# Moving the modulation rows of layer 1 out of the pair stages of a hybrid diffusion block's MLP

## The chip, the cores and the metric

The kernel runs on one core of a Trainium2 chip. The metric is the device time of one execution in microseconds (us); lower is better.

## The reference, cut to what matters

Two layers work on 512 latent tokens of width 1024. Each layer computes six modulation vectors of the conditioning vector, applies a mixer and then an MLP with squared ReLU. All of it is in 32-bit floats.

```python
for i in range(DEPTH):                      # DEPTH = 2
    mod_l = split(silu(c) @ ada_w[i] + ada_b[i], 6)          # 6 x 1024 numbers per layer
    a_lat = rmsnorm(h_lat, norm1_g[i]) * (1 + mod_l[1]) + mod_l[0]
    y_lat = mixer_i(a_lat)                  # i = 0: attention and long convolution; i = 1: pooling
    h_lat = h_lat + mod_l[2] * y_lat
    n = rmsnorm(h_lat, norm2_g[i]) * (1 + mod_l[4]) + mod_l[3]
    h_lat = h_lat + mod_l[5] * (square(relu(n @ mlp_w1[i])) @ mlp_w2[i])
return rmsnorm(h_lat, final_g)
```

The change concerns `mod_l` of layer 1: 6 x 1024 numbers, each a dot product of 1024 terms.

## The kernel before, in words

Tokens lie along the free dimension and channels on the 128 partitions, so that an activation of 1024 channels is eight tiles of 128x512. Every product of 32-bit numbers is made of rounded high parts and remaining low parts: high by high, high by low, low by high. So each weight tile of 128x1024 is loaded (`raw`, L182), rounded to its high part (`whi`, on ACT, L165) and subtracted to give its low part (`wlo`, on POOL in four pieces at L171, or on DVE in one at L173).

**The MLP** (`mlp`, from L1646) runs in each layer over four blocks of 1024 hidden channels, `blk` 0 to 3. A block has a *first map* (activations by `w1`, eight output tiles f = 0 to 7, squared ReLU in between) and a *second map* (by `w2`, eight output tiles d = 0 to 7, each added to the residual stream by `h_add`, L1582, with the gate `mods[layer, 5]`).

- In block 0 the first map has four tiles in halves and then four *whole tiles* f = 4 to 7 (`proj`, 24 matmuls of 512 columns). Its second map also makes sums of the activations (`act_sums`, L1657: five steps on DVE, one sum and four low parts on POOL, for d = 0 to 3), which blocks 1 to 3 use.
- In blocks 1 to 3 the first map is done in four *pairs* (`pair7`, L1721): two output tiles from seven half-size products instead of eight, with sums of two weight tiles in place of some tiles. A pair has 84 matmuls of 256 columns (L1681, L1682 and L1684). `pair_sums` (L1433; L1439 and L1440) makes weight sums on DVE, `pair_first` (L1446) others on POOL, and `pair7` itself asks DVE for the low part of one more weight (`w2 = w_split(..., dve)`), which PE needs in the fourth product.
- The second map of block 3 is `residual_norm` (L1598): four whole tiles, then four in halves, with the next norm's sums of squares beside them.

**Weights** are numbered k in the order of their use. `w_next` (L1477) fetches up to k + 7 and prepares up to k + 2; `w_more` does one ahead. Even k take a buffer of the ring `sraw` (four buffers), odd k one of `traw` (three).

**Modulation rows.** A row is one 128x1024 slice of layer 1's modulation matrix: `g_fetch` (L1489) loads it (512 KB, issued by SP at L1494) into a buffer of the same ring `sraw`, `grow` (L1499) multiplies it with the broadcast silu(c) and sums along the row (DVE, L1511, then a read of the accumulator), and `ada_fin` adds the bias (L254) or forms the scale (L249), in one more small DVE step. There are 48 rows, eight per vector, in the order of the six vectors (`gq`). `grow` has at most one row in flight beyond the one that it works on, and `glim` says up to which row it may go.

Nothing reorders the instructions: each engine does them in the order of the program text, SP too. An SP load whose buffer is still in use holds up all loads behind it. Before the change all 48 rows stand in layer 0's MLP: 8 in block 0's second map (two after each of d = 4 to 7), one after each pair of blocks 1, 2 and 3, and 14 in each of the second maps of blocks 1 and 2 (two after d = 0 to 5, one after d = 6 and 7).

Of the kernel before, what the change touches and what calls it, by code (L numbers as in the profile page):

```python
# [93 lines left out]
def body(ctx: ExitStack, tc: tile.TileContext, I, out):  # L94
# [1326 lines left out]

    pairs, first_done, sums_done, scr = set(), set(), set(), [None]

    def w_split(k, src, eng, n=1024):
# [35 lines left out]
    def w_prep(n):  # L1462
        while len(wsp) < min(n, len(wsrc)):
            k = len(wsp)
            if k in pairs:
                pair_first(k)
                wsp.append(w_split(k, wraw[k], pool))
            elif k - 1 in pairs:
                pair_sums(k - 1)
                wsp.append(w_split(k, scr[0][:, : 2 * T], dve))  # L1470
            else:
                eng = (dve, pool)[k // 2 % 2]
                wsp.append(wload(None, pool if k in fast else eng, "st"[k % 2], wraw[k]))

    wk = [0]
# [18 lines left out]
            nc.sync.dma_start(out=g, in_=I["adaT"][layer, c * D + j * P : c * D + (j + 1) * P, :])  # L1494
            gin.append(g)

    gk, glim = [0], [len(gq)]

    def grow(n=1):  # L1499
        for _ in range(n):  # L1500
# [97 lines left out]
    def residual_norm(kh, kl, gate, nrm, mod_a, d0=0, hook=None, late=0):  # L1598
# [3 lines left out]
        for d in range(d0, 4):  # L1602
            w = w_next()
            pp = ps_m("r")
            proj(pp, w, kh, kl, late=late if d == d0 else 0)
            h_add(d, 0, T, pp, gate)
            if hook and d == d0 + 1:
                hook()
            while fin:
                fin.pop(0)()  # L1610
            fin.append(nrm.add(d, 0, T))
# [34 lines left out]
    def mlp(layer, ah_, al_, nrm, i_norm, shift_in, last_norm, mod_next, load=None, seven=True):  # L1646
# [3 lines left out]
        if seven:  # L1650
            th = ml.tile([P, 4, 2, 3, 256], F32R, name=nm("th"), tag="pth")
            scr[0] = ml.tile([P, 2048], F32, name=nm("scr"), tag="ptl")
            pairs.update(k0 + 16 * blk + f for blk in (1, 2, 3) for f in (0, 2, 4, 6))


# [29 lines left out]
        for blk in range(4):  # L1685
# [89 lines left out]
            if blk == 0:  # L1775
# [21 lines left out]
                wait = pair(0, n, {16: mid0, 28: mid1} if layer == 0 else {48: mid0})  # L1797
                wait += pair(2, n, {} if layer == 0 else {8: mid1})
                steps(gb_[0])
                for f in range(4):  # L1800
                    w = ws[f]
                    pp = f_tile(f)
                    proj(pp[:, :n], w, ah_, al_, 256, n)
                    wait.append(lambda f=f, pp=pp: f_out(f, 256, n, pp))
                    wait.pop(0)()
                    w_more()
                while wait:
                    wait.pop(0)()
            if blk and seven:
                fin7 = lambda part: None  # L1810
                glim[0] = min(gk[0] + 4, len(gq))
                for f in range(0, 8, 2):
                    while len(gin) < min(gk[0] + 1, glim[0]):
                        g_fetch()
                    fin7 = pair7(f, fin7)
                    grow()
                fin7(3)
            else:
                for f in range(f0, 8):
                    w = w_next()  # L1820
                    pp = f_tile(f)
                    proj(pp, w, ah_, al_)
                    f_out(f, 0, T, pp)
            if blk < 3:
                glim[0] = min(gk[0] + (8 if blk == 0 else 14), len(gq))
                for d in range(ND):
                    if d == (0 if blk else 3):
                        while len(gin) < min(gk[0] + 2, glim[0]):
                            g_fetch()
                    w = w_next()  # L1830
                    pp = ps_m("r")
                    proj(pp, w, gh, gl, late=2 if blk and seven and d == 0 else 0)
                    h_add(d, 0, T, pp, gate)
                    if seven and blk == 0 and d < 4:
                        act_sums(d)
                    grow((0 if d < 4 else 2) if blk == 0 else (1 if d > 5 else 2))
            else:
                residual_norm(gh, gl, gate, last_norm, mod_next, hook=load, late=2 if seven else 0)

# [328 lines left out]
```

## Time and profile before

| what | value |
|---|---|
| time, median of 3 runs | 1125.92 us (1122.36 to 1126.22) |
| the profiled execution's own time | 1125.44 us |
| its span on the core, first to last instruction | 1123.6 us |
| mean granted TensorE clock | 0.987 of 2.4 GHz |
| PE (TensorE matmul) busy | 1068.5 us, 95% of the span |
| DVE (VectorE) busy | 792.2 us, 71% |
| POOL (GpSimd) busy | 677.5 us, 60% |
| ACT (ScalarE) busy | 522.6 us, 47% |

Times in the profile count from the first instruction. A row of a timeline gives start, duration, engine, line, operation, tiles and, in square brackets, how long the engine stood still just before and what ended it. PE's matmuls overlap, so that a row of one matmul is longer than the distance to the next. The chain of waits goes back from the last instruction through what released each step. A wait is put down to the instruction that came last.

### The profile page before, as it was taken

What the parts mean: (1) busy time and instruction counts of PE and PEld (TensorE: products, weight loads), DVE (VectorE), ACT (ScalarE), POOL (GpSimd) and SP (SyncE); (2) the same over time, 40 slices, a digit from 0 to 9 for tenths busy, and PEclk for the clock granted to TensorE, in tenths of its full rate; (3) what the DMA queues carried; (4) which work ended last, traced back from release to release, by engine and by line L of the source; (5) the groups of instructions that cost most, each with busy time, mean ns of one, the idle gap of its engine ahead of it and who ended that gap; (6) DMA issues with size and microseconds to landing.
All of it is one profiled execution on the core that took longest, in us unless ns stands there. A gap on an engine that the chain in (4) does not pass through costs nothing.

```text
span 1123.6 us, 17467 instructions
## 1 busy us (share of the span) xinstructions
PE 1068.5 (95%) x6604; PEld 942.8 (84%) x6604; DVE 792.2 (71%) x1258; ACT 522.6 (47%) x892; POOL 677.5 (60%) x723
## 2 busy tenths in 40 slices
PE   8899999999999999699999989999999999999996
PEld 5488888788989987688898888999878988988986
DVE  6689899999855547697798787386456934834843
ACT  4455245666544532273164155366433732732741
POOL 4457337885665449686596386476478834844822
PEclk9899999999999999899999999999999999999998
DMA  9776654225432323447736745521322341341302
GB/s 334 277 267 204 235 189 150 60 69 177 145 142 76 114 94 124 138 147 238 236 131 219 248 131 184 210 76 39 113 76 77 112 142 53 108 147 52 106 34 76
DMA packets 48664, 161.53 MB, mean 144 GB/s; under 512 B 5250, under 2 KB 8578, under 8 KB 48452
## 3 DMA queue, kind: packets, MB, share of 16 engines
q1 hardware_dynamic: 46132, 149.93, 39.6%
q0 software_dynamic: 2448, 10.49, 2.7%
q8 instruction: 52, 0.85, 0.3%
q14 instruction: 32, 0.26, 0.1%
HBM read 156.20 MB, written 4.20 MB: 143 GB/s over the span
## 4 chain that ended last, share of the span: by engine, by line
PE 57%; DVE 23%; DMA 8%; POOL 5%; issue 3%; ACT 3%; SPq 0%; POOLq 0%; ACTq 0%; DVEq 0%
PE r L206 7%; PE r L208 7%; PE r L212 7%; DMA g<-in_adaT 6%; PE f L1684 5%; PE f L1681 4%; PE f L1682 4%; DVE wlo L173 3%; DVE g L1511 3%; DVE g L638 3%; PE f L208 2%; PE f L212 2%; PE f L206 2%; DMA g<-in_adaN 1%; ACT whi L165 1%
## 5 line engine op out<-in xcount | busy, mean ns | idle before, releaser
L171 POOL TENSOR_TENSOR wlo<-raw,whi 128x256 fp32r<-128x256 f32 x308 | 265.1, 892 | 153.8 <-ACT whi L165 153.7
L206 PE MATMUL r<-gh,whi 128*128 128x512 f32 (+1 forms) x576 | 207.6, 369 | 1.6 <-ACT whi L165 1.5
L208 PE MATMUL r<-gl,whi 128*128 128x512 f32 (+1 forms) x576 | 207.0, 368 | 0.0
L165 ACT CAST whi<-raw 128x1024 fp32r<-128x1024 f32 x135 | 139.5, 1042 | 77.9 <-PE r L208 66.1
L1582 DVE SCALAR_TENSOR_TENSOR h<-r,mods,h 128x512 f32<-128x512 f32 (+1 forms) x81 | 54.0, 668 | 112.8 <-PE r L212 112.6
L212 PE MATMUL r<-gh,wlo 128*128 128x512 f32 (+1 forms) x576 | 132.0, 369 | 1.4 <-POOL wlo L171 1.4
L206 PEld LDWEIGHTS r<-gh,whi 128*128 128x128 f32 x576 | 108.3, 188 | 21.7 <-ACT whi L165 2.9
L208 PEld LDWEIGHTS r<-gl,whi 128*128 128x128 f32 x576 | 108.4, 188 | 18.6
L165 ACT CAST whi<-scr 128x1024 fp32r<-128x1024 f32 (+1 forms) x48 | 40.1, 835 | 175.7 <-DVE scr L1440 137.4
L212 PEld LDWEIGHTS r<-gh,wlo 128*128 128x128 f32 x576 | 100.2, 188 | 21.6 <-POOL wlo L171 3.0
L171 POOL TENSOR_TENSOR wlo<-scr,whi 128x256 fp32r<-128x256 f32 x48 | 60.4, 1278 | 74.0 <-ACT whi L165 51.3
L1681 PE MATMUL f<-nh,whi 128*128 128x256 f32 x384 | 95.3, 281 | 0.0
L1682 PE MATMUL f<-nl,whi 128*128 128x256 f32 x384 | 95.2, 281 | 0.0
L173 DVE TENSOR_TENSOR wlo<-raw,whi 128x1024 fp32r<-128x1024 f32 x58 | 73.8, 1272 | 13.9 <-ACT whi L165 13.9
L1511 DVE CUSTOM_DVE_ANT_0 g<-g,sbcl 128x1024 f32<-128x1024 f32 x48 | 63.5, 1323 | 21.7 <-DMA g<-in_adaT 21.6
L1681 PE MATMUL f<-th,whi 128*128 128x256 f32 x288 | 73.6, 287 | 3.1 <-ACT whi L165 3.1
L1682 PE MATMUL f<-th,whi 128*128 128x256 f32 x288 | 73.4, 286 | 0.0
L1681 PEld LDWEIGHTS f<-nh,whi 128*128 128x128 f32 x384 | 72.8, 189 | 0.2
L1682 PEld LDWEIGHTS f<-nl,whi 128*128 128x128 f32 x384 | 72.6, 189 | 0.3
L1684 PE MATMUL f<-th,wlo 128*128 128x256 f32 x288 | 49.4, 295 | 18.3 <-DVE wlo L173 18.2
L734 POOL TENSOR_TENSOR wlo<-raw,whi 128x1024 fp32r<-128x1024 f32 x17 | 43.1, 2533 | 38.3 <-ACT whi L725 37.9
L206 PE MATMUL u<-ah,whi 128*128 128x512 f32 x160 | 63.3, 396 | 1.1 <-DVE v L893 1.1
(415 smaller groups left out, 2812.1 us busy)
## 6 DMA issues: line engine op xcount, KB each, us to landing
raw<-in_w SPq DMA_DIRECT2D x128, 512.0 KB, 4.5
g<-in_adaT SPq DMA_DIRECT2D x80, 512.0 KB, 4.0
g<-in_adaN SPq DMA_DIRECT2D x16, 512.0 KB, 8.7
raw<-in_w_hy SPq DMA_DIRECT2D x12, 512.0 KB, 4.4
raw<-in_w_qk SPq DMA_DIRECT2D x8, 512.0 KB, 4.1
pth<-in_pth POOLq DMA_DIRECT2D x4, 768.0 KB, 9.1
raw<-in_w_out SPq DMA_DIRECT2D x5, 512.0 KB, 4.1
x<-in_xT SPq DMA_DIRECT2D x8, 256.0 KB, 7.2
```

Of the source, the lines that this page charges most:

```text
L165: act.copy(out=hi, in_=src)
L171: pool.tensor_tensor(out=lo[:, r], in0=src[:, r], in1=f32(hi)[:, r], op=ALU.subtract)
L173: (lo_eng or dve).tensor_tensor(out=lo, in0=src, in1=f32(hi), op=ALU.subtract)
L206: pe.matmul(ps, wh[:, c], ah[i][:, t0 : t0 + n], start=(i == 0), stop=False)
L208: pe.matmul(ps, wh[:, c], al[i][:, t0 : t0 + n], start=False, stop=False)
L212: pe.matmul(ps, wl[:, i * P : (i + 1) * P], ah[i][:, t0 : t0 + n], start=False, stop=(i == k - 1))
L734: ew(pool if k else dve).tensor_tensor(out=wts[k][1], in0=raws[k], in1=f32(wts[k][0]), op=ALU.subtract)
L1511: dve.tensor_tensor_reduce(out=gin[k], in0=gin[k], in1=sbc[0], scale=1.0, scalar=0.0, op0=ALU.mult, op1=ALU.add, accum_out=mods[:, layer, ...
L1582: dve.scalar_tensor_tensor(out=hs[d][:, seg], in0=pp[:, :n], scalar=gate[:, d : d + 1], in1=hs[d][:, seg], op0=ALU.mult, op1=ALU.add)
L1681: pe.matmul(o, l, b[i][0], start=(i == 0), stop=False)
L1682: pe.matmul(o, l, b[i][1], start=False, stop=False)
L1684: pe.matmul(o, w[1][:, c + i * P : c + (i + 1) * P], b[i][0], start=False, stop=(i == 3))
```

## The change

1. Rows no longer stand after pairs. Their places now are the whole tiles of block 0's first map (one after each of f = 4 to 7: the new `grow()` behind `f_out`), the second maps, and d = 0 to 3 of `residual_norm` (one each).
2. A helper `rows(n)` sets the limit to n more rows and starts the loads of the first two. In layer 0 it is called with 4 (before the halves of f = 0 to 3 in block 0), 8 (at d = 2 of block 0's second map, where it was d = 3), and 13, 13 and 4 (between the last pair of blocks 1, 2 and 3 and that pair's end). So layer 0 does 42 rows. The second maps of blocks 1 and 2 have two rows after d = 0 to 5, one after d = 6 and none after d = 7.
3. The last six rows go to layer 1's block 0: four beside its whole tiles, one after d = 0 and one after d = 1 of its second map. They belong to the gate, whose entries 2 to 7 are first read at d = 2 to 7 of that map.
4. `beside` names the first five weights of block 0's second map in each layer; their low parts are all on DVE. Before, POOL made two of them in layer 0 and three in layer 1.

```diff
+    beside = set()
...
-                eng = (dve, pool)[k // 2 % 2]
+                eng = dve if k in beside else (dve, pool)[k // 2 % 2]
...
-    gk, glim = [0], [len(gq)]
+    gk, glim = [0], [0]
+
+    def rows(n):
+
+        glim[0] = min(gk[0] + n, len(gq))
+        while len(gin) < min(gk[0] + 2, glim[0]):
+            g_fetch()
...
             proj(pp, w, kh, kl, late=late if d == d0 else 0)
             h_add(d, 0, T, pp, gate)
+            grow()
             if hook and d == d0 + 1:
...
             scr[0] = ml.tile([P, 2048], F32, name=nm("scr"), tag="ptl")
+            beside.update(range(k0 + 8, k0 + 13))
...
                 steps(gb_[0])
+                rows(4)
                 for f in range(4):
...
                 fin7 = lambda part: None
-                glim[0] = min(gk[0] + 4, len(gq))
                 for f in range(0, 8, 2):
-                    while len(gin) < min(gk[0] + 1, glim[0]):
-                        g_fetch()
                     fin7 = pair7(f, fin7)
-                    grow()
+                rows((13, 13, 4)[blk - 1])
                 fin7(3)
...
                     f_out(f, 0, T, pp)
+                    grow()
             if blk < 3:
-                glim[0] = min(gk[0] + (8 if blk == 0 else 14), len(gq))
                 for d in range(ND):
-                    if d == (0 if blk else 3):
-                        while len(gin) < min(gk[0] + 2, glim[0]):
-                            g_fetch()
+                    if blk == 0 and d == (0 if layer else 2):
+                        rows(8)
                     w = w_next()
...
-                    grow((0 if d < 4 else 2) if blk == 0 else (1 if d > 5 else 2))
+                    grow((layer if d < 4 else 2) if blk == 0 else 2)
```

Lines behind the first insertion move by 1 to 9 (L1511 is L1518 after the change, L1582 is L1589, L1439 is L1440).

**DVE, layer 0, from the last tiles of block 1's second map into the first pair of block 2.** `h` rows are `h_add`, `scr` rows are `pair_sums`, `ISA g` and `ISA mods` with the small step behind them are one modulation row, `wlo<-raw` behind them is the low part that PE's fourth product waits for. Before:

```order
L1439 TENSOR_TENSOR scr_3941<-raw_5508,raw_5468 128x512
L1440 TENSOR_TENSOR scr_3941<-scr_3941,raw_5468 128x512
L173 TENSOR_TENSOR wlo_5682<-scr_3941,whi_5681 128x1024
L1582 SCALAR_TENSOR_TENSOR h_3501<-r_5685,mods,h_3501 128x512
L1511 ISA g_5673,mods<-g_5673,sbcl 128x1024
L1511 ISA mods 128x1
L254 TENSOR_TENSOR mods<-mods,prm 128x1
L173 TENSOR_TENSOR wlo_5722<-raw_5508,whi_5721 128x1024
L1740 TENSOR_TENSOR r_5738<-f_5733,na_5735 128x256
```

And with the change:

```order
L1440 TENSOR_TENSOR scr_3941<-raw_5502,raw_5462 128x512
L1441 TENSOR_TENSOR scr_3941<-scr_3941,raw_5462 128x512
L173 TENSOR_TENSOR wlo_5674<-scr_3941,whi_5673 128x1024
L1589 SCALAR_TENSOR_TENSOR h_3501<-r_5677,mods,h_3501 128x512
L173 TENSOR_TENSOR wlo_5710<-raw_5502,whi_5709 128x1024
L1749 TENSOR_TENSOR r_5726<-f_5721,na_5723 128x256
```

The three rows of one modulation row between `h_add` and the low part are gone; the same holds at block 3 and behind every pair.

**DVE, layer 0, the last tile of block 0's second map and the first pair of block 1,** with the change:

```order
L1589 SCALAR_TENSOR_TENSOR h_3501<-r_4779,mods,h_3501 128x512
L1518 ISA g_4767,mods<-g_4767,sbcl 128x1024
L1518 ISA mods 128x1
L249 SCALAR_TENSOR_TENSOR smul<-mods,gpre,prm 128x1
L1518 ISA g_4805,mods<-g_4805,sbcl 128x1024
L1518 ISA mods 128x1
L249 SCALAR_TENSOR_TENSOR smul<-mods,gpre,prm 128x1
L173 TENSOR_TENSOR wlo_4818<-raw_4591,whi_4817 128x1024
```

Here nothing moved but the rows' numbers: before, two modulation rows stand at the same place, with L254 for L249, and the loads on SP around them stand in the same order too.

**DVE, layer 1, the first tile of block 0's second map.** `b` rows are `act_sums`. With the change:

```order
L1589 SCALAR_TENSOR_TENSOR h_3494<-r_8617,mods,h_3494 128x512
L1669 TENSOR_TENSOR b_8643<-nh_7993,nl_8001 128x512
L1671 TENSOR_TENSOR b_8645<-b_8643 128x256
L1672 TENSOR_TENSOR b_8645<-b_8644,b_8643 128x256
L1673 SCALAR_TENSOR_TENSOR b_8643<-b_8645,b_8643 128x256
L1674 SCALAR_TENSOR_TENSOR b_8644<-b_8643,b_8644 128x256
L1518 ISA g_8607,mods<-g_8607,sbcl 128x1024
L1518 ISA mods 128x1
L254 TENSOR_TENSOR mods<-mods,prm 128x1
L173 TENSOR_TENSOR wlo_8665<-raw_8487,whi_8664 128x1024
```

The last four rows are new on DVE at this place: before, the next `h_add` followed the five `act_sums` rows at once, and POOL made that low part ahead of its own `act_sums` steps.

## Rows read from the trace of the kernel before

**Rows 1.** The page, part 4: the chain that ended last, by engine.

```profile
PE 57%; DVE 23%; DMA 8%; POOL 5%; issue 3%; ACT 3%; SPq 0%; POOLq 0%; ACTq 0%; DVEq 0%
```

**Rows 2.** Stretches: length, busy us (instructions) of PE, weight load, DVE, ACT, POOL; clock, DMA, GB/s.

```profile
452.30:508.09 55.79, 44.10 (x337) 43.16 (x336) 46.03 (x69) 26.92 (x40) 39.97 (x37) 0.91 0.42 142
...
552.28:597.59 45.31, 40.76 (x337) 39.89 (x336) 41.36 (x62) 26.92 (x40) 35.52 (x32) 1.00 0.45 152
...
641.78:689.51 47.73, 42.62 (x337) 41.54 (x336) 42.20 (x66) 26.93 (x40) 35.01 (x32) 0.96 0.44 148
...
858.98:899.02 40.04, 40.04 (x337) 39.79 (x336) 32.79 (x49) 25.86 (x39) 36.09 (x36) 1.00 0.32 106
```

**Rows 3.** PE's waits (us in total, times, longest), layer 0's pairs of blocks 1, 2, 3.

```profile
PE f L1684 <- DVE wlo L173: 8.6, 3, 6.0
PE f L1681 <- ACT whi L165: 3.1, 1, 3.1
...
PE f L1684 <- DVE wlo L173: 4.5, 4, 1.6
...
PE f L1684 <- DVE wlo L173: 5.1, 4, 2.2
```

**Rows 4.** Timeline of DVE and PE, end of the third pair of block 1, layer 0.

```profile
500.14 1.45 DVE L1511 CUSTOM_DVE_ANT_0 g<-g,sbcl 128x1024 f32<-128x1024 f32 x1
502.12 1.21 DVE L173 TENSOR_TENSOR wlo<-raw,whi 128x1024 fp32r<-128x1024 f32 x1
...
503.39 0.73 PE L1684 MATMUL f<-th,wlo 128*128 128x256 f32 x4 [1.63 <-DVE wlo L173]
```

**Rows 5.** Timeline of DVE and PE where the pairs of blocks 2 and 3 begin.

```profile
555.88 1.54 DVE L1511 CUSTOM_DVE_ANT_0 g<-g,sbcl 128x1024 f32<-128x1024 f32 x1
557.95 1.21 DVE L173 TENSOR_TENSOR wlo<-raw,whi 128x1024 fp32r<-128x1024 f32 x1
...
559.22 0.74 PE L1684 MATMUL f<-th,wlo 128*128 128x256 f32 x4 [1.46 <-DVE wlo L173]
...
649.78 1.10 PE L1684 MATMUL f<-th,wlo 128*128 128x256 f32 x4 [2.15 <-DVE wlo L173]
```

**Rows 6.** Timeline of DVE, PE and SP's queue where the pairs of block 1 begin.

```profile
448.84 2.73 SPq L1494 DMA_DIRECT2D g<-in_adaT  x2
...
453.20 1.78 DVE L1511 CUSTOM_DVE_ANT_0 g<-g,sbcl 128x1024 f32<-128x1024 f32 x1 [1.38 <-DMA g<-in_adaT]
...
465.63 1.29 DVE L1511 CUSTOM_DVE_ANT_0 g<-g,sbcl 128x1024 f32<-128x1024 f32 x1 [3.18 <-DMA g<-in_adaT]
...
458.52 0.39 PE L1681 MATMUL f<-th,whi 128*128 128x256 f32 x1 [3.09 <-ACT whi L165]
...
468.70 1.22 PE L1684 MATMUL f<-th,wlo 128*128 128x256 f32 x4 [6.02 <-DVE wlo L173]
```

**Rows 7.** The page, part 5 (busy us, mean ns; idle before): low parts and rows on DVE.

```profile
L173 DVE TENSOR_TENSOR wlo<-raw,whi 128x1024 fp32r<-128x1024 f32 x58 | 73.8, 1272 | 13.9 <-ACT whi L165 13.9
L1511 DVE CUSTOM_DVE_ANT_0 g<-g,sbcl 128x1024 f32<-128x1024 f32 x48 | 63.5, 1323 | 21.7 <-DMA g<-in_adaT 21.6
```

**Rows 8.** DVE's waits in layer 1, 778 to 853 us: block 0, both maps.

```profile
DVE r L1699 <- ACT gh L1698: 16.4, 7, 4.2
DVE b L1663 <- POOL b L1661: 5.8, 2, 3.3
```

**Rows 9.** PE's wait in layer 1's block 0, second map, and DVE's idle time there.

```profile
PE r L206 <- ACT whi L165: 1.2, 1, 1.2
...
853.86 0.75 DVE L1582 SCALAR_TENSOR_TENSOR h<-r,mods,h 128x512 f32<-128x512 f32 x1 [3.02 <-PE r L212]
```

**Rows 10.** Timeline of DVE, layer 0's `residual_norm`, d = 2.

```profile
706.47 0.75 DVE L1582 SCALAR_TENSOR_TENSOR h<-r,mods,h 128x512 f32<-128x512 f32 x1 [4.77 <-PE r L212]
```

**Rows 11.** Timeline of DVE and POOL, layer 1's block 0, second map, a low part.

```profile
840.97 1.59 DVE L173 TENSOR_TENSOR wlo<-raw,whi 128x1024 fp32r<-128x1024 f32 x1 [1.48 <-ACT whi L165]
...
841.45 2.27 POOL L1661 TENSOR_TENSOR b<-nh,nl 128x512 f32<-128x512 f32 x1
```

## The prediction

> **What bounds the kernel now.** First the chain of waits, summed by engine: PE has 57% of the span and DVE 23% [rows 1]. PE is busy for 95% of the span, so a change can only win where PE stands still or runs at a low clock. Second, the windows cut at the stages that lose rows. The five pair stages shown do the same matmuls, 337 each [rows 2]. Layer 1's pairs, which have no modulation rows beside them, take 40.04 us, and PE is busy for all of it. Layer 0's, with a row behind each pair, take 55.79, 45.31 and 47.73. Taking 40.04 as the floor, the excess is 15.75 + 5.27 + 7.69 = 28.7 us, and this is the only room the pair stages offer. Third, who stopped PE there: nearly always L1684, PE's fourth product of a pair, waiting for DVE's low part at L173: 8.6, 4.5 and 5.1 us in the three blocks, plus one wait of 3.1 for ACT's high part [rows 3].
>
> The waits do not fill the whole excess. In block 2 the clock is 1.00 and PE's busy time is 40.76, 0.72 over the floor after four waits: a refill of 0.18 each. Block 1 has four waits too, and its busy time is 44.10: 4.06 - 0.72 = 3.3 us are left, which belong to a granted clock of 0.91 (part of the stretch at 1.2 GHz). Block 3: 42.62 - 40.04 - 0.72 = 1.9 us at a clock of 0.96. So block 1 pays 11.7 in waits, 0.7 in refills and 3.3 in clock; block 2 pays 4.5 + 0.7; block 3 pays 5.1 + 0.7 + 1.9.
>
> **The change, part by part.** *Rows leave the pairs.* At the end of block 1's third pair the low part starts at 502.12, and PE's product at 503.39 after 1.63 us of standing still [rows 4]. What ran on DVE just before it is a modulation row; where block 2 begins one can be measured, from 555.88 to 557.95: 2.07 us with its two small steps [rows 5]. Without the row the low part comes 2.07 earlier, as long as its high part is there (the bound is layer 1's stage, where the same program without rows has no wait). So each wait shorter than 2.07 goes, with its refill.
>
> - Block 2: the wait of 1.46 at its first pair [rows 5] came behind d = 7's row, which goes; the three behind pairs go too. All 4.5 + 0.7: **-5.3**, to the floor.
> - Block 3: its first pair's wait is 2.15 [rows 5], again behind d = 7's row; 0.1 stays. Block 2 waited 1.46 and kept its clock, so with 0.1 I expect block 3 to keep it: **-7.6**.
> - Block 1: its waits of 3.09 and 6.02 [rows 6] are another matter. They come behind d = 7's rows of block 0, which stay, in the same order on DVE. Two row loads left SP at 448.84; DVE waited 1.38 us for data at 453.20 and 3.18 at 465.63 [rows 6]. A load can only go when the buffer of an earlier row is free, and loads, rows and weights stand in the same order on SP after the change (the first two loads one tile earlier, at d = 2). I therefore leave both waits and the 3.3 of clock. Two steady waits go: 8.6 - 6.0 = 2.6, with 0.36 of refill: **-2.9**. The other end: all 15.75.
>
> *Where the rows go.* The second maps of blocks 1 and 2 have one row fewer and otherwise the same ones: 0. Six rows and three low parts come to DVE in layer 1's block 0. A low part is 1.27 on the mean [rows 7], so that is 6 x 2.07 + 3 x 1.27 = 16.2 us of new DVE work. DVE stood still there for 16.4 us in seven waits for ACT's squares, up to 4.2 each, and 5.8 for POOL's sums [rows 8]: 22.2 us of cover, and a row of 2.07 fits behind each whole tile. Without that cover it would be late for the next block. POOL loses three tiles, ACT's high part of d = 6 gets its buffer sooner, and the 1.2 us wait of PE [rows 9] goes with its refill: **-1.4**; the bounds are 0 and -1.4, and I take the upper gain because DVE still has 3.02 us of idle time before h_add at 853.86 [rows 9]. Four rows beside layer 0's whole tiles have the same cover as layer 1's: 0. Four in `residual_norm`: DVE idles 4.77 us before a tile's `h_add` [rows 10] against 2.07 of row: 0, or up to +3.3 if a wait there cost the clock as in block 1.
>
> A DVE low part took 1.59 us, against 1.27 on the mean, while POOL's sum of two 128x512 tiles at 841.45 took 2.27 [rows 11]. The Trainium skill (SBUF — State Buffer, Who interferes with whom) says that a DVE instruction with two SBUF inputs contends with a GpSimd instruction that reads SBUF, and that whoever issues second is blocked. By that rule the low parts and rows moved beside POOL's sums would stretch both engines, and layer 1's 1.4 could be lost: the sum would be 1.4 worse. The row agrees in direction, with 0.32 us.
>
> *SP.* Each row's load goes ahead of weight loads at three new places (whole tiles in either layer, `residual_norm`). I cost this at nothing, since weights are fetched seven ahead; if that cover were gone, block 1's entry shows the price (below).
>
> **Sum:** 5.3 + 7.6 + 2.9 + 1.4 = 17.2 us. From the profiled execution's 1125.44 that is **1108.2 us**. That execution lies 0.5 under the median of 1125.92, so the two starts are the same.
>
> **Rivals.**
>
> *Entries stay (1114.0).* The first pair of blocks 2 and 3 is late for another reason than the row, for example because d = 7's `h_add` itself comes late from PE. Then only the steady waits go: block 1's 2.9; block 2's 4.5 - 1.46 + 0.54 = 3.6; block 3's 5.1 - 2.15 + 0.54 = 3.5; layer 1's 1.4; together 11.4. For it: at the end of a map PE is the last to be done with d = 7. Against: the low part comes right behind a row, and the wait is about as long as one.
>
> *Block 1's entry goes too (1095.4).* Loads one tile earlier let rows run ahead, so the wait of 6.02 does not build up: 15.75 in place of 2.9. Against: the last loads still wait for the rows before them.
>
> *SP holds weights back (1148).* At each of the three new places a row load stuck on a buffer keeps the weights behind it, and PE waits as at block 1's entry: 3.1 + 6.0 + 0.36 + 3.3 = 12.8 us each, 38.4 in all against 15.8 gained in the pairs, so 22.6 slower. It ends slower once a place costs over 5.3. For it: block 1's entry is such a place, with eight rows. Against: there two rows stand behind each tile, here one.
>
> *DVE overflows in layer 1 (1129).* The 16.2 us find no cover and come out at the next block's entry with 3.3 of clock: 15.8 gained, 19.5 lost, 1129.1. The cover of 22.2 us speaks against it.
>
> *The change does not do what it says (1124).* If ACT's high part ends the wait rather than the row, the low part is no earlier and only layer 1's 1.4 comes. For it: DVE stood still 13.9 us for high parts in its low parts [rows 7]. Against: layer 1's pairs.
>
> **How the numbers follow.** My forecast has a chance of 0.64, with 1104 (a third of block 1's entry gained) to 1111.5 (`residual_norm` at its upper bound) as its own range. Entries stay: 0.16. Block 1's entry goes too: 0.08. SP holds weights: 0.04. DVE overflows: 0.02. The high part decides: 0.06. The first two together hold 0.80, so the range is 1101 to 1117, where the upper end is the second case with 3 us from `residual_norm`, and the lower the forecast with somewhat over half of block 1's entry. A measurement of this kernel tells about 0.5%, 5.6 us. Faster by more: 0.64 + 0.16 + 0.08 = 0.88. Within: 0.02 + 0.06 = 0.08. Slower: 0.04.
>
> **What would show it.** Right: layer 0's pair stages at about 53, 40 and 40 us; waits of L1684 for DVE's low part only at block 1's entry (about 6 us, behind ACT's 3.1) and at most 0.1 at block 3's; a granted clock of 1.00 in block 3 and below 1 in block 1; no wait of 1.2 us in layer 1's block 0; DVE's busy time higher and POOL's lower there. Wrong in its parts: waits of 1.5 to 2 us still at the first pairs of blocks 2 and 3 (entries stay); block 1 at 40 (the lower case); PE waiting for `whi` or DMA in a whole tile or in `residual_norm` (SP); a lag of `h_add` growing through layer 1's block 0, with a wait at its block 1 (overflow). Most of all the prediction is wrong if layer 0's pairs keep waits like the 1.63 us with no row before the low part.

## The result and the profile after

The changed kernel takes **1110.88 us** (median of 4 runs, 1108.43 to 1113.27), the kernel before in the same comparison 1124.79 (4 runs, 1122.36 to 1126.22): a ratio of **0.9878**, interval 0.9848 to 0.9909. The forecast was 1108.2, range 1101 to 1117. The profiled executions have spans of 1123.6 and 1110.1 us, 13.5 apart.

The windows of the changed kernel, with the columns of [rows 2]: layer 0's second map of block 0, its pairs of blocks 1, 2 and 3, its last map (`residual_norm` up to the halves), then layer 1's second map of block 0.

```profile
405.70:452.55 46.85, 45.47 (x194) 35.68 (x193) 35.22 (x52) 14.17 (x25) 34.61 (x33) 1.00 0.46 157
452.55:505.16 52.61, 43.50 (x337) 43.04 (x336) 40.33 (x60) 26.89 (x40) 35.32 (x37) 0.90 0.37 120
549.35:591.43 42.08, 40.83 (x338) 39.96 (x337) 36.38 (x55) 26.90 (x40) 32.31 (x32) 1.00 0.37 126
635.61:676.61 41.00, 40.52 (x337) 39.93 (x336) 36.02 (x54) 26.90 (x40) 32.23 (x32) 1.00 0.35 120
676.61:712.43 35.82, 35.45 (x206) 30.98 (x205) 19.04 (x31) 13.28 (x20) 22.76 (x29) 1.00 0.74 279
800.93:845.46 44.53, 44.44 (x194) 35.97 (x193) 34.27 (x47) 15.61 (x27) 32.60 (x32) 1.00 0.38 129
```

The kernel before, for the three maps that [rows 2] does not show:

```profile
405.21:452.30 47.09, 45.44 (x194) 35.66 (x193) 32.59 (x47) 14.18 (x25) 39.24 (x39) 1.00 0.38 123
689.51:724.43 34.92, 34.92 (x206) 30.85 (x205) 13.39 (x22) 13.36 (x20) 19.70 (x28) 1.00 0.65 238
812.90:858.98 46.08, 44.77 (x194) 35.89 (x193) 26.10 (x35) 15.73 (x27) 34.14 (x40) 1.00 0.20 69
```

Stage by stage, in us, against [rows 2] and these three:

| stage | before | after | difference | forecast |
|---|---|---|---|---|
| layer 0, block 0, second map | 47.09 | 46.85 | -0.24 | 0 |
| pairs of block 1 | 55.79 | 52.61 | -3.18 | -2.9 |
| pairs of block 2 | 45.31 | 42.08 | -3.23 | -5.3 |
| pairs of block 3 | 47.73 | 41.00 | -6.73 | -7.6 |
| last map of layer 0 | 34.92 | 35.82 | +0.90 | 0 |
| layer 1, block 0, second map | 46.08 | 44.53 | -1.55 | -1.4 |
| sum | | | -14.03 | -17.2 |

The first of these stages begins 0.49 us later in the profile of after (405.70 against 405.21), which makes the 13.5. Between profiles this point moves by some us: in those below it lies from 401.3 to 408.7. That arises ahead of all that the kernels place differently, since the stretch just ahead, which ends with the whole tiles, the first of those places, takes 33.5 us in each of them. So the experiments are read by the lengths of stages, and the medians beside them.

PE's waits in the three pair stages of layer 0, which answer to [rows 3]:

```profile
PE f L1693 <- DVE wlo L173: 6.0, 1, 6.0
PE f L1690 <- ACT whi L165: 3.1, 1, 3.1
...
PE f L1690 <- ACT whi L165: 0.8, 1, 0.8
PE f L1693 <- DVE wlo L173: 0.4, 1, 0.4
```

Block 1 keeps its two entry waits unchanged, and nothing else. Block 2 has a new wait, 0.8 for ACT's high part, and 0.4 for the low part; block 3 has a wait of 0.4 for the low part alone. All steady waits behind pairs are gone.

Where block 2 begins, on DVE and PE (timeline of after; the row of before that answers to the first stands last):

```profile
547.28 1.23 DVE L1518 CUSTOM_DVE_ANT_0 g<-g,sbcl 128x1024 f32<-128x1024 f32 x1 [4.71 <-DMA g<-in_adaT]
...
550.62 0.69 DVE L1440 TENSOR_TENSOR scr<-raw,raw 128x512 f32<-128x512 f32 x1
...
553.24 0.39 PE L1690 MATMUL f<-th,whi 128*128 128x256 f32 x1 [0.77 <-ACT whi L165]
...
556.61 0.75 PE L1693 MATMUL f<-th,wlo 128*128 128x256 f32 x4 [0.42 <-DVE wlo L173]
...
547.79 1.23 DVE L1511 CUSTOM_DVE_ANT_0 g<-g,sbcl 128x1024 f32<-128x1024 f32 x1 [2.53 <-DMA g<-in_adaT]
```

The second row of d = 5 waited 4.71 us for its data, where it had waited 2.53. Counted from the start of that map it ran 547.28 - 505.16 = 42.1 us in, against 547.79 - 508.09 = 39.7 before [rows 2]: 2.4 later. Behind it stand `h_add`, d = 6's row and `pair_sums`, on which ACT's high part waits. The rows ahead of it stand within 0.6 us of their old places. Its load left SP no later, 35.4 us behind the start of the map against 35.2 before, but the wait for it ended 6.7 us after it left, where that had taken 4.5. The two loads, after and before:

```profile
540.60 0.33 SPq L1495 DMA_DIRECT2D g<-in_adaT  x1
...
543.29 0.33 SPq L1494 DMA_DIRECT2D g<-in_adaT  x1
```

### The profile page after: what moved, and what is told of

It reads as the page before. It is cut to its first block, busy times and chain, and to the rows that moved or that the text cites. A ratio compares the mean times of both kernels' runs of the same rounds, so it can differ in the third digit from the quotient of the medians.

```text
span 1110.1 us, 17472 instructions
## 1 busy us (share of the span) xinstructions
PE 1066.5 (96%) x6604; PEld 941.5 (85%) x6604; DVE 797.0 (72%) x1263; ACT 522.1 (47%) x892; POOL 658.6 (59%) x703
## 4 chain that ended last, share of the span: by engine, by line
PE 60%; DVE 19%; DMA 11%; ACT 3%; POOL 3%; issue 3%; SPq 0%; POOLq 0%; ACTq 0%; DVEq 0%
DMA g<-in_adaT 8%; PE f L1693 7%; PE f L1690 7%; PE f L1691 7%; PE r L206 6%; PE r L208 6%; PE r L212 6%; DVE g L1518 3%; DVE g L638 3%; PE f L208 2%; PE f L212 2%; PE f L206 2%; DVE wlo L173 2%; DMA g<-in_adaN 1%; DVE h L1589 1%
## 5 line engine op out<-in xcount | busy, mean ns | idle before, releaser
L171 POOL TENSOR_TENSOR wlo<-raw,whi 128x256 fp32r<-128x256 f32 x288 | 246.9, 888 | 123.8 <-ACT whi L165 123.8
L1589 DVE SCALAR_TENSOR_TENSOR h<-r,mods,h 128x512 f32<-128x512 f32 (+1 forms) x81 | 54.0, 668 | 100.3 <-PE r L212 100.1
L171 POOL TENSOR_TENSOR wlo<-scr,whi 128x256 fp32r<-128x256 f32 x48 | 56.5, 1198 | 72.1 <-ACT whi L165 48.4
L173 DVE TENSOR_TENSOR wlo<-raw,whi 128x1024 fp32r<-128x1024 f32 x63 | 82.7, 1312 | 12.3 <-ACT whi L165 12.3
L1518 DVE CUSTOM_DVE_ANT_0 g<-g,sbcl 128x1024 f32<-128x1024 f32 x48 | 63.8, 1329 | 26.1 <-DMA g<-in_adaT 25.2
L208 PE MATMUL u<-al,whi 128*128 128x512 f32 x160 | 62.6, 391 | 0.0
```

Of the source, the lines that this page charges most:

```text
L171: pool.tensor_tensor(out=lo[:, r], in0=src[:, r], in1=f32(hi)[:, r], op=ALU.subtract)
L173: (lo_eng or dve).tensor_tensor(out=lo, in0=src, in1=f32(hi), op=ALU.subtract)
L208: pe.matmul(ps, wh[:, c], al[i][:, t0 : t0 + n], start=False, stop=False)
L1518: dve.tensor_tensor_reduce(out=gin[k], in0=gin[k], in1=sbc[0], scale=1.0, scalar=0.0, op0=ALU.mult, op1=ALU.add, accum_out=mods[:, layer, ...
L1589: dve.scalar_tensor_tensor(out=hs[d][:, seg], in0=pp[:, :n], scalar=gate[:, d : d + 1], in1=hs[d][:, seg], op0=ALU.mult, op1=ALU.add)
```

## Experiments

Two theories were on the table. **Work:** a row is 2 us of DVE work, and PE waits where it stands ahead of a low part. **Data:** DVE stands still ahead of a row because the row's load waited on SP for a buffer of the shared ring. They agree about pairs and differ about entries.

### early: four rows moved away from block 1's entry

```diff
-                rows(4)
+                rows(4 if layer else 6)
...
-                    grow()
+                    grow(2 if blk == 0 and layer == 0 and f < 6 else 1)
...
-                        rows(8)
+                        rows(8 if layer else 4)
...
-                    grow((layer if d < 4 else 2) if blk == 0 else 2)
+                    grow((layer if d < 4 else (2 if d < 6 else 0)) if blk == 0 else 2)
```

> The changed kernel, with the four rows of d = 6 and 7 in layer 0's block 0 moved: two go behind the whole tiles f = 4 and 5 of the same block, two to layer 1 (one after each of d = 0 to 3 there). Theory: block 1's entry (waits of 3.09 and 6.02 us and the low clock, 12.6 us over the floor of 40.0) comes from these rows, whose data arrive late in front of pair_sums and of the low part. Then both waits fall below 1 us, block 1's pair stage goes from 52.6 to 40 to 42 us, and the kernel to 1098 to 1101 us. Rival: the entry comes from pair_sums and the weights' own loads, whatever stands on DVE: then the pair stage stays over 50 us and the kernel at 1110. Second rival: DVE lags behind the whole tiles, with two rows there; then block 0's second map grows from 46.8 by over 2 us.

Measured: 1096.22 us, ratio 0.9741 (0.9705 to 0.9777). Layer 0's pairs of blocks 1 and 2 (block 3's take 40.01) and layer 1's second map of block 0:

```profile
452.01:492.56 40.55, 40.02 (x337) 39.77 (x336) 34.16 (x50) 26.90 (x40) 36.16 (x36) 1.00 0.34 118
536.74:577.18 40.44, 40.25 (x337) 39.81 (x336) 34.79 (x51) 26.88 (x40) 32.27 (x32) 1.00 0.34 118
...
783.94:829.29 45.35, 44.47 (x194) 35.97 (x193) 37.90 (x52) 14.54 (x26) 34.70 (x30) 1.00 0.45 150
```

Block 1 falls from 52.61 to 40.55 with the clock at 1.00: these four rows, with their loads, were its whole entry, waits and low clock. The rivals fall: the stage is not over 50 us, and block 0's second map stays at 46.8. The price: the two rows added behind d = 2 and 3 of layer 1 cost 0.8 there (45.35 against 44.53). Blocks 2 and 3 gained as well (42.08 to 40.44, 41.00 to 40.01), which the edit did not aim at. The entries thus depend on more than the rows that stand there.

### own_buffer: same order, other buffers

```diff
-            g = st.tile([P, D], F32, name=nm("g"), tag="sraw", bufs=4)
+            g = (ml.tile([P, D], F32, name=nm("g"), tag="gr", bufs=1) if k % 2 else
+                 st.tile([P, D], F32, name=nm("g"), tag="sraw", bufs=4))
```

> The changed kernel, in the same order, but every second row is loaded into a buffer of its own instead of the ring that it shares with the weights. Theory: what holds DVE at block 1's entry is less the rows' work than their loads, which wait for a buffer of the ring: DVE stood still 1.7, 1.8 and 3.2 us for row data there, 6.6 in all, against 9.1 us of waits of PE. Then these idle times shrink to 2 us or less in all, PE's two waits to 3 to 5 us, block 1's pair stage from 52.6 to 44 to 48, block 2's from 42.1 to 40 to 41, and the kernel to 1103 to 1107 us. Rival: the rows' work on DVE alone sets it, and an earlier load changes nothing: 52 to 53 us and 1110.

Measured: 1101.46 us, ratio 0.9782 (0.9751 to 0.9813). Block 0's second map, the pairs of blocks 1 and 2, the last map of layer 0; then DVE's waits for row data from 425 to 470 us, here and in the changed kernel:

```profile
402.49:450.68 48.19, 46.81 (x194) 36.79 (x193) 36.88 (x55) 14.18 (x25) 35.94 (x34) 0.96 0.47 150
450.68:498.04 47.36, 43.05 (x337) 42.39 (x336) 39.13 (x58) 27.19 (x40) 34.14 (x36) 0.93 0.39 132
542.22:581.93 39.71, 39.71 (x337) 39.66 (x336) 33.21 (x49) 25.67 (x39) 31.06 (x32) 1.00 0.39 141
665.81:700.73 34.92, 34.92 (x206) 30.85 (x205) 18.18 (x31) 13.12 (x20) 19.77 (x28) 1.00 0.72 265
...
DVE g L1519 <- DMA g<-in_adaT: 1.8, 1, 1.8
```

```profile
DVE g L1518 <- DMA g<-in_adaT: 6.6, 3, 3.2
```

DVE's idle time for row data falls by 4.8 us and block 1's pairs by 5.25, as the data theory has it. Block 2 goes to the floor (39.71 with PE busy throughout, 0.3 under the prediction's 40.04) and the last map back to 34.92: the 0.90 lost there were late data too. Block 0's map grew by 1.3 us, at a clock of 0.96 (the last section comes back to it). The 47.36 that is left in block 1 holds the rows' own work, the 1.8 us that DVE still waits for data, and the low clock (0.93): PE still waits 3.9 us for the low part and 0.4 for the high part. So at this entry both theories hold: about 5 us go to late data, and the 7 to 8 that are left were not split further.

### pair_rows_2: rows behind the pairs of block 2 again

```diff
                 fin7 = lambda part: None
+                if blk == 2:
+                    rows(4)
                 for f in range(0, 8, 2):
                     fin7 = pair7(f, fin7)
-                rows((13, 13, 4)[blk - 1])
+                    if blk == 2:
+                        grow()
+                rows((13, 9, 4)[blk - 1])
```

> The changed kernel with one part undone in one block: block 2 has a row behind each of its four pairs again, and its second map four rows fewer. Theory: a row of about 2 us between h_add or pair_sums and the low part makes PE's waits, as before the change: 0.5, 0.9 and 1.6 us return inside the stage with 0.18 us of refill each, and the stage goes from 42.1 to about 45.6 us; block 3's entry has fewer rows before it and loses its 0.4. Kernel 1113 to 1114. Rival: the pairs gained for another reason (POOL's lower load, loads of weights in time), and the stage stays within 0.5 us of 42.1.

Measured: 1113.24 us, ratio 0.9893 (0.9864 to 0.9921), 2.4 over the changed kernel; the intervals of the two ratios overlap, so the stages decide. Pairs of block 2 (block 3's take 39.74), and PE's waits there:

```profile
549.74:594.70 44.96, 41.24 (x337) 40.04 (x336) 40.98 (x63) 26.91 (x40) 35.37 (x32) 1.00 0.44 151
...
PE f L1693 <- DVE wlo L173: 3.7, 4, 1.6
```

The waits return, 1.6 the longest as in [rows 3, 4], and block 3 with four rows fewer ahead of it goes to the floor. Three of the four waits stand behind rows, 0.7, 0.9 and 1.6 us; none of these rows waited for its data. So work alone explains the steady waits.

### pool_low_parts: the change without its fourth part

```diff
-            beside.update(range(k0 + 8, k0 + 13))
```

> The changed kernel without its fourth part: the low parts of the first weights of block 0's second map are shared between DVE and POOL again, the rows stay where they are. Theory: the wait of 1.2 us in layer 1's block 0 went because POOL makes fewer low parts: it returns, and that map goes from 44.5 back to 46 us; layer 0's goes from 46.8 to about 47.1. Rows on DVE behind d = 0 and 1 may add to it, as POOL's low parts then come after the same sums: up to 48. Kernel 1111.5 to 1114. Rival: it went for another reason, and both maps stay within 0.3 us.

Measured: 1112.59 us, ratio 0.9892 (0.986 to 0.9924). Second maps of block 0, layers 0 and 1, and PE's wait in the second of them:

```profile
406.05:453.84 47.79, 45.45 (x194) 35.67 (x193) 35.56 (x50) 14.17 (x25) 41.65 (x40) 1.00 0.45 154
798.72:846.85 48.13, 46.09 (x194) 37.10 (x193) 31.93 (x45) 15.86 (x27) 36.20 (x40) 0.96 0.36 121
...
PE r L206 <- ACT whi L165: 2.0, 1, 2.0
```

Layer 1's map goes to 48.13, over the 46.08 of before: the wait of 1.2 [rows 9] comes back as 2.0, with the clock at 0.96. The fourth part is needed to place rows there; it is worth 3.6 us in layer 1 and 0.9 in layer 0 as the rows now stand. The median moves by 1.7 only, and the intervals of the two ratios overlap: in the profile block 2 has no entry wait here (its pairs take 40.2). The row load that took 6.7 us in the changed kernel took 5.1.

### d7_row: a row at d = 7 again

```diff
-                    grow((layer if d < 4 else 2) if blk == 0 else 2)
+                    grow((layer if d < 4 else 2) if blk == 0 else (1 if d in (0, 6, 7) else 2))
```

> The changed kernel with one row moved in each of the second maps of blocks 1 and 2: from d = 0 to d = 7, where a row stood before the change. Theory: the entries of blocks 2 and 3 are set by what stands on DVE behind d = 6 and 7; the row returns 1.5 to 2 us of wait there. Block 2's pair stage goes from 42.1 to 43.5 to 44.2 us, block 3's from 41.0 to 42.5 to 44.9 (the upper end with the clock falling as before the change), the kernel to 1113 to 1116. Rival: the entries shrank because the pairs before them no longer leave DVE behind, and the row at d = 7 costs under 0.5 us in each block.

Measured: 1117.41 us (10 runs, 1112.16 to 1123.12), ratio 0.9936 (0.9909 to 0.9962). Pairs of block 2 (block 3's take 44.40, at the same clock), and PE's wait there (the same in both):

```profile
548.35:592.70 44.35, 42.04 (x337) 41.38 (x336) 37.98 (x57) 27.02 (x40) 31.97 (x32) 0.96 0.38 129
...
PE f L1693 <- DVE wlo L173: 2.1, 1, 2.1
```

The low part's entry waits return, 1.7 more than the 0.42 of the changed kernel, and the clock falls as it did in block 3 before the change. That is what the prediction said of a row at d = 7. The kernel is over the expected 1116 for two stages more: `residual_norm`, 36.55 in place of 35.82, and block 0's map, 48.36 in place of 46.85. This map lies ahead of the edit and has the same instructions and waits as in the changed kernel; only its clock was lower, 0.96.

### before_own: the kernel before, with the other buffers

The edit is that of own_buffer, in the kernel before.

> The kernel before the change, rows at their old places, every second row in a buffer of its own. It tells whether places or loads made the loss. Theory: the steady waits behind pairs are DVE's work on a row and stay (0.9 and 1.6 in block 1, 0.5 to 1.6 in blocks 2 and 3); only the entry of block 1 gets shorter, by about 5 us as in own_buffer. Pair stages 50 to 51, 44.5 to 45.3 and 46 to 47.7 us; kernel 1118 to 1121. Rival: late loads make all of it, and an extra buffer would have done what the change does: pair stages of blocks 2 and 3 at 40 to 41 and the kernel at 1112 or less.

Measured: 1117.01 us (7 runs), ratio 0.992 (0.9896 to 0.9943). Pairs of blocks 1 and 2 (block 3's take 43.68) and PE's waits in block 2:

```profile
458.35:506.90 48.55, 42.21 (x338) 41.42 (x336) 43.04 (x66) 26.92 (x40) 38.11 (x35) 0.96 0.47 152
551.07:594.76 43.69, 40.51 (x337) 39.84 (x336) 40.45 (x61) 25.52 (x39) 35.52 (x32) 1.00 0.46 147
...
PE f L1685 <- DVE wlo L173: 3.2, 3, 1.6
```

The three steady waits stay, as expected. But the entries of blocks 2 and 3 are gone although d = 7's row stands there as before the change: with data in time DVE reaches it early enough. Together with d7_row: **late data and a row at d = 7 make these entries late together**. Without the late data nothing was left of them here; without the row most went, with stages of 42.08 and 41.00 in the changed kernel and 40.44 and 40.01 in early. More than the expected share of block 1's entry went as well (48.55), but block 0's map grew from 47.09 to 49.68 (the last section says why).

### early_own and early_own_low6: both edits together, and one low part more on DVE

early_own has both diffs; in the second kernel, besides:

```diff
-            beside.update(range(k0 + 8, k0 + 13))
+            beside.update(range(k0 + 8, k0 + 14))
```

> Both edits on the changed kernel: the four rows of d = 6 and 7 in block 0 moved (early), and every second row in a buffer of its own (own_buffer). Theory: the two take away the same entry waits in different shares and add up only in what is left. Against early, the pair stages of layer 0 lose 0.7, 0.7 and 0.3 us (to the 39.7 to 39.9 of layer 1), the last map of layer 0 0.3: 1093 to 1095 us, 1 to 3 under early. Rival: a new wait, the own buffer still held by the row two before, which DVE reaches late behind two rows in each of the whole tiles f = 4 and 5: then block 0's second map grows past 48.2, or weights come late, and the kernel is no faster than early (1096).

> As early_own, with one weight more in the list of those whose low parts DVE makes (six of block 0's second map in place of five), in both layers. Theory: PE's two waits of 0.4 and 0.9 us in layer 0's block 0, second map, are for low parts that POOL makes behind its own sums; with 3.0 us less on POOL ahead of them both go, and the map falls from 46.8 to 44.2 to 45.5 us; kernel 1 to 2.5 us under early_own. Rival: DVE, which makes sums there as well, holds the next high part's buffer longer, and a new wait of 1 us or more for ACT's high part comes in its place: no gain, or up to 2 us slower.

Measured: early_own 1101.02 us, ratio 0.9782 (0.9742 to 0.9821); early_own_low6 1095.28 us, ratio 0.972 (0.9673 to 0.9768). Block 0's second map of early_own, then PE's waits in it; the map of early_own_low6 last:

```profile
406.45:456.80 50.35, 48.31 (x194) 37.50 (x193) 36.80 (x52) 16.70 (x28) 38.10 (x37) 0.93 0.38 121
...
PE r L212 <- POOL wlo L171: 2.0, 3, 0.9
```

```profile
407.40:452.73 45.33, 44.72 (x194) 35.90 (x193) 36.64 (x52) 14.10 (x25) 32.29 (x30) 1.00 0.42 130
```

early_own was expected under early and came out 5 us over it (the intervals of the two ratios overlap, so the stages have to show why). All pair stages of layer 0 stand at the floor (39.73, 39.70, 39.70), but block 0's map grew from 46.8 to 50.35: a third wait for POOL's low part and the clock at 0.93. The named rival (a map past 48.2) came, though not through the rows of the whole tiles. The last section says what POOL did. One low part less for POOL brings the map to 45.33; as a kernel that is level with early.

### spread and spread_ring: no rows in layer 0's block 0 map

Beside early_own_low6: `rows(15)`, `rows(15)`, `rows(6)` in place of 13, 13, 4, no `rows` in layer 0's block 0 map, `grow(2 if d < 2 else 1)` in `residual_norm`. spread_ring has all rows in the shared ring.

> A version meant to be the best: as early_own_low6, but block 0's second map of layer 0 has no rows; its four go to the second maps of blocks 1 and 2 (15 each: two after d = 0 to 6, one after d = 7) and the two of layer 1 behind d = 2 and 3 to the last map of layer 0 (six: two after d = 0 and 1, one after d = 2 and 3). Theory: rows with their data in time cost only where DVE is late: block 0's map 44.2 to 45.3, no wait at block 1's entry (40.6 to 39.9), layer 1's map 44.5; the entries of blocks 2 and 3 stay without a wait although a row stands at d = 7, as in before_own: pair stages 39.7. Kernel 1090 to 1094, 1 to 4 under early_own_low6. Rival: 15 rows are one too many, d = 7's row returns waits of 1 to 2 us in both blocks (43 to 44 us each): 1097 to 1101.

> The same places as in spread, all rows in the ring that they share with the weights. It tells whether a row at d = 7 costs through its work or through late data. Theory from before_own (own buffer: entries of blocks 2 and 3 at no wait with a row at d = 7) and d7_row (ring: 2.15 in each): the data are late, so here blocks 2 and 3 have waits of 1.5 to 3 us at their entries and pair stages of 43 to 45 us, against 39.7 to 41 in spread; block 1's entry has no wait in either. Kernel 1098 to 1103. Rival: places alone decide, and both kernels have the same pair stages within 0.5 us.

Measured: spread 1102.02 us, ratio 0.9782 (0.975 to 0.9814); spread_ring 1107.05, ratio 0.9828 (0.9805 to 0.985). spread: block 0's map, the pairs of block 2 (block 3's take 41.88), the last map, and DVE's waits for row data from 491 to 540 us, block 1's map. spread_ring: the pairs of block 2 (block 3's take 44.57):

```profile
407.36:451.55 44.19, 44.19 (x194) 36.05 (x193) 29.98 (x41) 16.15 (x28) 31.14 (x33) 1.00 0.26 86
...
535.44:577.93 42.49, 40.29 (x337) 39.83 (x336) 37.08 (x57) 26.90 (x40) 32.33 (x32) 1.00 0.38 130
663.99:702.67 38.68, 35.56 (x206) 31.03 (x205) 21.32 (x37) 13.28 (x20) 22.14 (x29) 1.00 0.72 269
...
DVE g L1519 <- DMA g<-in_adaT: 1.8, 2, 1.6
```

```profile
531.57:577.79 46.22, 42.04 (x338) 41.38 (x336) 38.52 (x57) 27.04 (x40) 31.96 (x32) 0.96 0.39 127
```

The rival of the first came: 15 rows are one too many (42.49 and 41.88), and six in the last map cost 3.8 us. But the data were not in time everywhere, although every second row has its own buffer: the second row of d = 6 waited 1.6 us for them in block 1's map and 1.0 in block 2's, and three rows of the last map 9.3 together. So this cost is work and loads in one. In the shared ring blocks 2 and 3 take another 3.7 and 2.7 us. Block 0's map without rows is at 44.19, with no wait at all, and block 1's entry is gone.

### balanced and balanced_low5: each place loaded up to what it hides

Beside spread: 14, 14 and 4 rows in place of 15, 15 and 6; two rows in each of layer 0's whole tiles; six beside layer 1's whole tiles. The diff is against the changed kernel. balanced_low5 has five low parts on DVE, as the changed kernel.

```diff
-                rows(4)
+                rows(6 if layer else 8)
...
-                    grow()
+                    grow(2 if blk == 0 and (layer == 0 or f < 6) else 1)
...
-                    grow((layer if d < 4 else 2) if blk == 0 else 2)
+                    grow(layer if blk == 0 else (2 if d < 6 else 1))
```

> The version meant to be the best, after spread: every second row in a buffer of its own, six low parts on DVE, no rows in layer 0's second map of block 0; layer 0 has eight rows beside the whole tiles (two each), 14 in each of the second maps of blocks 1 and 2 (two after d = 0 to 5, one after d = 6 and 7, as before the change), four in the last map; layer 1 has six beside its whole tiles and one after d = 0 and 1. Theory: a place costs only where rows and their loads exceed what DVE has left before PE needs the next low part; 14 with the own buffer left no wait in before_own, 4 in the last map none in own_buffer. Against spread (1099.2 us of span) the pair stages of blocks 2 and 3 go from 42.5 and 41.9 to 39.7 and the last map from 38.7 to 34.9; all pair stages at 39.7 to 40.0, span 1090 to 1093, kernel 1091 to 1095. Rival: two rows in each whole tile overrun there, h_add lags and block 0's map of layer 0 grows by 2 us or more; then no faster than early (1096).

> As balanced, with five low parts on DVE, as in the changed kernel. It tells what made PE wait 0.4 and 0.9 us for POOL's low parts in layer 0's block 0: too many low parts on POOL, or rows on DVE that slow POOL's steps beside them. First theory: the waits return (1.4 us, map 46 to 47 in place of 44.2). Second theory: without rows there POOL's four pieces of a low part take 3.0 us in place of 4.8, and the map stays within 0.5 us of 44.2.

Measured: balanced **1093.64 us** (5 runs), ratio **0.9689** (0.9662 to 0.9716); balanced_low5 1095.46, ratio 0.9718 (0.9692 to 0.9745). balanced: block 0's map, the pairs of block 1 (those of blocks 2 and 3 take 39.86 and 39.89, the last map 34.92), and the second row of f = 7 on DVE. balanced_low5: block 0's map and PE's one wait in it:

```profile
401.26:446.71 45.45, 44.47 (x194) 36.00 (x193) 32.15 (x47) 15.63 (x27) 29.87 (x32) 1.00 0.33 116
446.71:486.63 39.92, 39.92 (x337) 39.79 (x336) 33.72 (x49) 25.59 (x39) 33.39 (x34) 1.00 0.39 137
...
407.21 1.23 DVE L1519 CUSTOM_DVE_ANT_0 g<-g,sbcl 128x1024 f32<-128x1024 f32 x1 [1.58 <-DMA g<-in_adaT]
```

```profile
405.89:452.58 46.69, 44.47 (x194) 35.96 (x193) 31.41 (x46) 15.70 (x27) 32.24 (x36) 1.00 0.33 112
...
PE r L206 <- ACT whi L165: 2.2, 1, 2.2
```

Every pair stage of layer 0 is under 40 us, PE busy throughout, and the ratios 0.9689 and 0.9878 put the kernel 1.9% of the time before below the changed one. What is left is 1.3 us in block 0's map, where PE waits 1.0 for ACT's high part. The trace shows where it comes from: the second row of the last whole tile, f = 7, waited 1.58 us for its data, so that `h_add` of d = 0 ran 8.5 us behind the start of the map, against 5.9 in spread; `act_sums` lag by as much behind it, and ACT makes the high part only after its steps on these sums. So the named rival came in part, through the load of the eighth row.

balanced_low5 does not decide its question. PE no longer waits for POOL's low parts, but it also reaches them later: the wait for the high part is 2.2 us here, with the row of f = 7 late by 1.2. POOL's four pieces ended 36.8, 38.5, 39.2 and 39.9 us behind the start of the map. PE's first product with them came at 39.5, and without its wait it would have come at about 37.3 (an estimate, 39.5 less 2.2), so that waits for POOL could have stood there. The pair early_own_low6 and spread answers it (last section). Between these two kernels the intervals overlap.

## Why the prediction was right, and where a size was off

**Right: the steady waits.** They went in all three blocks, and pair_rows_2 brought them back in one (0.7, 0.9 and 1.6 us) behind rows that had not waited for data; before_own keeps them although the loads come earlier. They are DVE's work on the row ahead of the low part.

**Right: block 1's entry stays.** The forecast kept 3.09, 6.02 and the clock; the trace has 3.1, 6.0 and 0.90. That d = 7's and d = 6's rows make it is shown by early (52.61 to 40.55), and that their late loads make a good part of it by own_buffer (to 47.36).

**Right: layer 1.** -1.55 against -1.4, and for the reason given: pool_low_parts loses it and more. The 16.2 us of new DVE work found their cover; the rival of an overflow did not come (the pairs behind that map take 39.9 us, PE busy throughout).

**Right: the clock of block 3.** With 0.4 us of wait at its entry it is 1.00.

**Off in size: block 2's entry, 2.0 us, and block 3's, 0.9.** The step that failed is that d = 7's row goes, the low part comes 2.07 earlier and all of the rest costs 0: "the second maps of blocks 1 and 2 have one row fewer and otherwise the same ones". The rows are the same, but the row ahead, d = 6's, can be late by itself, and then all behind it is: `pair_sums` came late and ACT's high part with it (0.77), then the low part (0.42). The traces order themselves by the start of d = 6's row behind the start of its map: 39.7 us in own_buffer (the next pair stage takes 39.71), 42.2 in pool_low_parts (40.16), 43.0 ahead of block 3 in the changed kernel (41.00) and 44.1 ahead of block 2 (42.08). That earlier loads take the entry away is shown by own_buffer, with the same rows in the same order. What made block 2's worse than block 3's is one load, which took 6.7 us; at the same place it took 4.1 to 5.1 in the other kernels with the shared ring. Why it was slow there stays open, and part of the 2.0 us may belong to the profiled execution alone.

**Off in size: the last map of layer 0,** +0.90 where 0 was taken from a span of 0 to 3.3. The cover of 4.77 us [rows 10] was enough for the rows' work; their data came 1.8 us late at one tile. With the own buffer the stage is back at 34.92.

These misses are one: the work of rows was priced at every place, the pace of their loads at block 1's entry alone. With 2.0, 0.9 and 0.9 taken off, the 17.2 us would have been 13.4.

The rival "entries stay" was partly right in its time (1114.0 against 1110.88) and wrong in its cause: it was not PE or `h_add` but row data. "SP holds weights back" did not come: in the windows of after PE waits for no DMA.

## What to carry to other kernels

Work that fills an engine's idle time has two prices: the time it takes there, and when its data come; an idle time can be long enough for the work and still be lost to its load. Ask of each moved step whose buffer its load waits for, and count its place from the start of the stage, not only what stands next to it. Fill each place only as far as it hides (with every second row in its own buffer, 14 rows in a map cost nothing and 15 cost 2 to 3 us; in the shared ring 13 cost up to 2) and keep such work away from an engine that another one waits for.

## What had not been expected

**Data in time made a stage slower.** In early_own rows no longer waited for data, and POOL's four pieces of a low part beside them took 5.87 us. The same four took 4.83 in the changed kernel, where the second of two rows comes too late to run beside them, 3.81 in balanced_low5 with no rows (a low part beside them), and 3.01 for a low part that POOL makes while DVE mostly waits. In before_own, too, they took 5.87, and PE had a third wait for them, 1.0 us. Timelines of POOL, in this order: early_own, the changed kernel twice, balanced_low5; then early_own_low6 and spread, which differ up to there by the rows of this map alone:

```profile
442.50 5.87 POOL L171 TENSOR_TENSOR wlo<-raw,whi 128x256 fp32r<-128x256 f32 x4
```

```profile
441.74 4.83 POOL L171 TENSOR_TENSOR wlo<-raw,whi 128x256 fp32r<-128x256 f32 x4
...
431.49 3.01 POOL L171 TENSOR_TENSOR wlo<-raw,whi 128x256 fp32r<-128x256 f32 x4
```

```profile
441.94 3.81 POOL L171 TENSOR_TENSOR wlo<-raw,whi 128x256 fp32r<-128x256 f32 x4
```

```profile
440.73 6.01 POOL L171 TENSOR_TENSOR wlo<-raw,whi 128x256 fp32r<-128x256 f32 x4
```

```profile
439.69 3.81 POOL L171 TENSOR_TENSOR wlo<-raw,whi 128x256 fp32r<-128x256 f32 x4
```

The rule of the Trainium skill that the prediction named (SBUF — State Buffer, Who interferes with whom) says that DVE instructions with two inputs in SBUF contend with GpSimd instructions that read it; these times agree with it. Its price fell at another place than the prediction said: layer 1's 1.4 us were not lost, while in layer 0's map, before the change as after it, rows stretch POOL's low parts. PE's wait for them there goes with the rows: 0.6 us in early_own_low6, none in spread.

**The same wait does not always move the clock.** In early_own block 0's map had 2.0 us of waits in three pieces and took 6.2 us more than the 44.19 of spread. Of the 4.1 beside the waits, 1.3 stand in the changed kernel's map too, behind two waits and at a clock of 1.00 (PE busy 45.47 against 44.19); the other 2.8 come with the third wait and with a clock that fell to its lower level, 1.2 GHz, for a time. In the changed kernel and in d7_row the same instructions of that map have the same two waits, 1.4 us together. Five us each from that place, the changed kernel and d7_row:

```profile
445.00:450.00 5.00, 4.07 (x17) 3.10 (x18) 3.24 (x7) 0.00 (x0) 5.00 (x6) 1.00 0.75 278
```

```profile
443.40:448.40 5.00, 4.07 (x11) 2.97 (x11) 2.87 (x6) 0.00 (x0) 5.00 (x6) 0.66 0.79 278
```

PE is busy for as long, but 11 matmuls are done in place of 17, at a granted clock of 0.66 in place of 1.00. This alone is 1.5 us between two executions of the same code. So 1.3 us of own_buffer's map, and some of early_own's, may be such a draw; in spread, where the map has no wait, the clock stayed at 1.00. A wait of 2.1 us at block 2's entry likewise left the clock at 1.00 in spread and at 0.96 in d7_row.
